# A hybrid convolution and attention block on one core: raw weights asked for two projections ahead, attention results in other slots, two rotation steps in front

## The chip, the core and the metric

The kernel runs on one core of a Trainium2 chip. What counts is the time of one execution on the device in microseconds (us), as the median of several runs. A core has five engines that run side by side, each with an instruction queue of its own: TensorE (PE in the profile, PEld for its weight loads), VectorE (DVE), ScalarE (ACT), GpSimd (POOL) and SyncE (SP), which here only issues DMA transfers. An instruction that waits holds up all that stand behind it on its engine.

## What is computed

The reference is a decoder block in float32 for 2048 tokens of width 1024:

```python
h = rmsnorm(x, norm_g[l])
proj = jnp.einsum("bsd,de->bse", h, w_in[l])
glu_in, conv_gate, q, k, v, attn_gate, merge_logits = jnp.split(proj, SPLIT_POINTS, axis=-1)
c = conformer_conv(glu_in, conv_dw_w[l], conv_dw_b[l], conv_ln_g[l], conv_ln_b[l])
y_conv = jnp.einsum("bsc,cd->bsd", c * jax.nn.silu(conv_gate), w_conv_out[l])
q = rope(q.reshape(B, S, N_Q_HEADS, HEAD_DIM), pos)
k = rope(k.reshape(B, S, N_KV_HEADS, HEAD_DIM), pos)
...
a = sliding_window_attention(q, k, v, sinks[l])
y_attn = jnp.einsum("bsa,ad->bsd", a * jax.nn.silu(attn_gate), w_attn_out[l])
g_conv, g_attn = jnp.split(jax.nn.sigmoid(merge_logits), 2, axis=-1)
x = x + jnp.einsum("bsd,de->bse", g_conv * y_conv + g_attn * y_attn, w_out[l])
return rmsnorm(x, final_norm_g)
```

(The gates' two lines are drawn into one here.) The convolution is a gated linear unit, a depthwise convolution over 31 tokens, a LayerNorm with scale and bias, and a SiLU. The attention has 16 query heads of 64 that share 4 key and value heads, a window of 128 tokens, and one sink per head in the softmax's denominator.

## The kernel before

**Sweeps and products.** The tokens are worked on in two sweeps of 1024, each as two halves of 512. Every float32 product is made of three matmuls in a rounded float32 form (`product`): a weight and an activation are each split into a rounded high part and what is left, the low part, and high x high, high x low and low x high are added up in PSUM. A projection (`project`) is one column group of 128 output columns: 2 halves x 8 slices of 128 inputs x 3 matmuls = 48 matmuls of 128x512. For the attention projection (names ya, on PE `mm_ya`), the convolution's (yc) and the gates (ag, cg, ma, mc) there are eight column groups each, written ya0_3 for sweep 0 and group 3. Queries come in pairs, q3_a and q3_b for the first and second half of the rotated vectors, ga and gb are the two inputs of the gated linear unit.

**Weights.** Each projection is an item with a prefetch and its blocks of matmuls. `Line.run` calls the prefetch of the next item and then runs the blocks of the held one, so the weights are asked for one item ahead. In `load_w` a group's weights come as two halves: SP issues the DMA of the raw weights (L273), ACT casts the high part (`whi`, L274), and in sweep 0 POOL makes the low part by a subtraction (`wlo`, L259), which is also stored to memory (`d_lo`, L290). In sweep 1 the low part is loaded from there (L276). The tiles raw, whi and wlo each have four buffers, that is, those of two projections.

**Order.** PE follows the program's order exactly. The other engines are ordered by a scheduler that knows priorities: `front()` (L326) lifts what is issued within it ahead of nearly all else, and the evacuation of a product from PSUM is lifted less. Three PSUM banks (`mm_ps`) take the projections' products in turn, so the fourth product can begin only when the first has been copied out.

**Slots.** Large tiles live in named slots: H and A for activations, C[0] to C[7] for the eight conv rows `cv`, X[0] to X[2] for three more. The DVE works on the convolution all through the projections; then comes its LayerNorm: the mean in X[0] (`ln_chain`, L934), `ln_chain2` (L946) with the reciprocal of the deviation in X[1], `ln_apply` (L930) with a multiply on DVE (L931) and a SiLU on ACT (L932) for each of the eight rows. `u_op` then multiplies row e, half by half, with its SiLU gate (`lcg`, L587) and splits the product into uT (cast L330 on ACT), the input of the convolution's projection; it notes ("u", e, half) as stored. X[2] is used by the attention's value tiles.

**The attention's projection.** `ya_item` evacuates column group e into mp[e], which takes the slot of conv row e. So it first lets the program issue all up to ("u", e, 1) (`line.until`), and its copies (L1037 on ACT) wait for the conv row to be used up. `yc_item` reads mp[e] (L1060), and the output projection's weights `wo` are loaded into C[0] to C[7] after that (`load_wo`, L1120).

**Queries and keys.** `rope_items` rotates them: `ev_a` and `ev_b` multiply a product by cosine and sine on DVE (tiles ra and rb, L603, L604, L609, L610), then POOL subtracts and adds (L611, L612), and the result is split (hq_a on ACT L652, hq_c on DVE L653) and stored to `d_q` by SP (L659), from where the attention loads it as `qk` (L755). The attention's scores (sc, L788) and its outputs (ov) lie on PE between the matmuls of the gates' projections; its normalized blocks are stored to `d_a`, and POOL's copies of the sinks into a block's tile (L794) wait for the stores of earlier ones.

Of the kernel before, what the change touches and what calls it, by code (L numbers as in the profile page):

```python
# [54 lines left out]
def hybrid_block(ctx: ExitStack, tc: tile.TileContext, x, xt, par_d, w_in, w_conv, sinks, w_attn, w_out,  # L55
# [202 lines left out]
    def split_lo(out_, full, hi, eng):  # L258
        return eng.tensor_tensor(out=out_, in0=full, in1=f(hi), op=ALU.subtract)  # L259

    def load_w(src, name, home=None, steps=None):

        parts = []
        at = lo_at.setdefault((src.tensor.name, src.offset), len(lo_at))

        def part(kh):
            if home is None:
                raw = stage.tile([P, 4, P], F32, tag="raw", name=f"raw_{name}{kh}")
                hi = stage.tile([P, 4, P], F32R, tag="whi", name=f"whi_{name}{kh}")
                lo = stage.tile([P, 4, P], F32R, tag="wlo", name=f"wlo_{name}{kh}")  # L270
            else:
                raw, hi, lo = (home[i][:, kh] for i in range(3))
            od(nc.sync.dma_start(out=raw, in_=src[:, 4 * kh:4 * kh + 4, :]))  # L273
            act.copy(hi, raw)  # L274
            if (at, kh) in lo_stored:
                od(nc.sync.dma_start(out=f(lo), in_=d_lo[at, kh]))  # L276
            else:
                split_lo(lo, raw, hi, dve if steps is not None else pool)
            parts.append((hi, lo))

        for kh in range(2):
            if steps is None:
                part(kh)
            else:
                steps.append(lambda kh=kh: part(kh))

        def keep(kh):
            if (at, kh) not in lo_stored:
                lo_stored.add((at, kh))
                nc.sync.dma_start(out=d_lo[at, kh], in_=f(parts[kh][1]))  # L290

        return lambda k: (parts[k // 4][0][:, k % 4, :], parts[k // 4][1][:, k % 4, :]), keep
# [9 lines left out]
    def project(src, rhs, name, evac, halves=(0, 1), small=False):  # L302

        got = {}

        def prefetch():
            got["w"] = load_w(src, name)

        def blocks():
            for half in halves:  # L310
                if small:
                    ps = small_bank(f"mm_{name}{half}")
                else:
                    ps = mm_ps.tile([P, TH], F32, tag="mm", name=f"mm_{name}{half}")
                for k in range(KC):
                    product(ps, got["w"][0](k), rhs(k, half), k)
                    if k == KC - 1:
                        with tc.high_priority(offset=PRIO):
                            evac(half, ps)
                    if half == halves[-1] and k % 4 == 3:  # L320
                        got["w"][1](k // 4)
                    yield 3 * MM_US

        return prefetch, blocks, (src, name, evac)

    def front():  # L326
        return tc.high_priority(offset=20 * PRIO)
# [175 lines left out]
    def sweep(s):  # L503
# [94 lines left out]
        def rope_items(name, e, store):  # L598
            first = {}

            def ev_a(half, ps):
                t = first[half] = slot(AT[4 + half], [P, 2, TH], F32, f"ra{s}_{name}_{half}")
                dve.tensor_tensor(out=t[:, 0, :], in0=ps, in1=cs[half][:, 0, :], op=ALU.mult)  # L603
                dve.tensor_tensor(out=t[:, 1, :], in0=ps, in1=cs[half][:, 1, :], op=ALU.mult)  # L604

            def ev_b(half, ps):
                a = first[half]
                b = slot(next_of("rb", [AT[6], AT[13]]), [P, 2, TH], F32, f"rb{s}_{name}_{half}")
                dve.tensor_tensor(out=b[:, 1, :], in0=ps, in1=cs[half][:, 1, :], op=ALU.mult)  # L609
                dve.tensor_tensor(out=b[:, 0, :], in0=ps, in1=cs[half][:, 0, :], op=ALU.mult)  # L610
                pool.tensor_tensor(out=a[:, 0, :], in0=a[:, 0, :], in1=b[:, 1, :], op=ALU.subtract)  # L611
                pool.tensor_tensor(out=a[:, 1, :], in0=a[:, 1, :], in1=b[:, 0, :], op=ALU.add)  # L612
                for i in range(2):
                    store(i, half, a[:, i, :])

            return [project(w_in[e], h_rhs, f"{name}a{s}", ev_a),
                    project(w_in[e + 1], h_rhs, f"{name}b{s}", ev_b)]
# [397 lines left out]
            glu_after = glu_after[2:]  # L1015
        for half in range(2):
            load_rope(half)
        for i, item in enumerate(others):
            todo = [item]
            if glu_after and i == glu_after[0]:  # L1020
# [3 lines left out]
                todo[0] = ahead(todo[0], start_attention)  # L1024
            if i == nqkv - 3:
                todo[0] = ahead(todo[0], prepare_v)
            yield from todo


        mp = {}  # L1030

        def ya_item(e, first):
            def ev(half, ps):
                if half == 0:
                    line.until(lambda: ("u", e, 1) in stored)
                    mp[e] = slot(C[e], [P, T], F32, f"mp{s}_{e}")
                act.copy(mp[e][:, half * TH:(half + 1) * TH], ps)  # L1037

            prefetch, blocks, _ = project(w_attn[e], lambda k, half: aT[half][k],
# [24 lines left out]

            return project(w_conv[e], lambda k, half: uT[half][k], f"yc{s}_{e}", ev)

        yield ya_item(0, True)
        for e in range(1, KC):
            yield ya_item(e, False)
        for e in range(KC):  # L1070
            yield yc_item(e)


        gb = work.tile([P, D], F32, tag="ln0", name=f"gb{s}", bufs=1)
# [182 lines left out]
```

## Time and profile before

| | us |
|---|---|
| median of 3 runs | 2004.92 (2004.77 to 2005.31) |
| the profiled execution's own time | 2003.76 |
| its span, first to last instruction | 2001.7 |
| PE busy | 1979.3 (99% of the span) |
| PEld busy | 1651.0 (82%) |
| DVE busy | 1305.1 (65%) |
| ACT busy | 982.1 (49%) |
| POOL busy | 434.3 (22%) |

The mean granted clock of TensorE was 0.996 of the full one. Rows of the timelines give the start and the duration in us, the engine, the line of the program, the operation with output and input names (buffer and group numbers left out), shapes, and how many instructions the row joins; brackets hold the idle time of the engine ahead of it and what ended that. A row "A <- B: total, times, longest" of the waits says that A waited for B. Matmuls are pipelined: a row of one can last 0.39 us while the next starts 0.23 us after it.

### The profile page before, as it was taken

How to read it: one execution, taken by the hardware profiler on the slowest of the kernel's cores; microseconds unless marked ns; L12 is line 12 of the kernel's file. 1: busy time of each engine (PE TensorE's matmuls, PEld its weight loads, DVE VectorE, ACT ScalarE, POOL GpSimd, SP SyncE). 2: the span in 40 equal slices, each digit the busy share in tenths (PEclk: the TensorE clock that was granted, in tenths of full speed). 3: DMA queues.
4: the chain of work that ended last, by engine and by line, in shares of the span. 5: the costliest groups of instructions: out<-in, count | busy, mean ns of one | idle time of the engine just before them, and what ended most of it. 6: DMA issues, size and time to landing. Idle time of an engine off the chain costs nothing.

```text
span 2001.7 us, 27128 instructions
## 1 busy us (share of the span) xinstructions
PE 1979.3 (99%) x9264; PEld 1651.0 (82%) x9264; DVE 1305.1 (65%) x1737; ACT 982.1 (49%) x2250; POOL 434.3 (22%) x462
## 2 busy tenths in 40 slices
PE   8999999999999998999999999999999999999998
PEld 6888788888888886888888888888888888888887
DVE  6998487787887546133858666787877875432434
ACT  7322567556555346234613126666565554553422
POOL 0445323423333242241001121111111110001200
PEclk9999999999999998999999999999999999999999
DMA  8566655655656844357537485556655677554632
GB/s 308 192 200 196 241 167 176 205 187 179 207 185 219 270 173 163 117 187 259 205 116 273 133 243 187 184 174 199 191 181 182 206 225 259 189 174 132 215 132 84
DMA packets 287545, 386.13 MB, mean 193 GB/s; under 512 B 22960, under 2 KB 138032, under 8 KB 287408
## 3 DMA queue, kind: packets, MB, share of 16 engines
q1 hardware_dynamic: 287408, 384.41, 57.7%
q8 instruction: 73, 1.20, 0.2%
q14 instruction: 64, 0.52, 0.1%
HBM read 252.20 MB, written 132.12 MB: 192 GB/s over the span
## 4 chain that ended last, share of the span: by engine, by line
PE 88%; DVE 1%; ACT 1%; SPq 0%; POOL 0%; DMA 0%; issue 0%; DVEq 0%; POOLq 0%; ACTq 0%
PE mm_cg L297 9%; PE mm_ma L297 9%; PE mm_mc L297 9%; PE o L1179 9%; PE mm_yc L297 9%; PE mm_ag L297 8%; PE mm_ya L297 8%; PE mm_ga L297 8%; PE mm_gb L297 7%; PE sc L788 3%; PE ov L847 2%; PE mm_q_a L297 2%; PE mm_q_b L297 2%; PE tpp L823 1%; PE mm_v L297 1%; PE mm_kb L297 1%
## 5 line engine op out<-in xcount | busy, mean ns | idle before, releaser
L526 DVE SCALAR_TENSOR_TENSOR acc<-glu,par,acc 128x1024 f32<-128x1024 f32 x464 | 595.6, 1284 | 7.4
L1179 PE MATMUL o<-wo,mT 128*128 128x512 f32 x768 | 174.8, 389 | 0.0
L1179 PEld LDWEIGHTS o<-wo,mT 128*128 128x128 f32 x768 | 144.2, 188 | 30.0
L297 PE MATMUL mm_ya<-aT,whi_ya 128*128 128x512 f32 x512 | 159.6, 393 | 7.5 <-ACT mp L1037 7.5
L297 PE MATMUL mm_cg<-hT,whi_cg 128*128 128x512 f32 x512 | 160.0, 394 | 0.0
L297 PE MATMUL mm_ma<-hT,whi_ma 128*128 128x512 f32 x512 | 160.0, 393 | 0.0
L297 PE MATMUL mm_ag<-hT,whi_ag 128*128 128x512 f32 x512 | 159.7, 393 | 0.0
L297 PE MATMUL mm_mc<-hT,whi_mc 128*128 128x512 f32 x512 | 158.3, 390 | 0.0
L297 PE MATMUL mm_yc<-uT,whi_yc 128*128 128x512 f32 x512 | 157.7, 389 | 0.0
L297 PE MATMUL mm_ga<-hT,whi_ga 128*128 128x512 f32 x448 | 139.7, 393 | 1.3 <-ACT whi_ga L274 1.3
L297 PE MATMUL mm_gb<-hT,whi_gb 128*128 128x512 f32 x448 | 139.5, 392 | 0.0
L811 ACT ACTIVATE ss<-ss,st 128x129 f32<-128x129 f32 x256 | 100.1, 394 | 60.7 <-DVE st L808 60.4
L297 PEld LDWEIGHTS mm_ya<-aT,whi_ya 128*128 128x128 f32 x512 | 97.1, 190 | 28.2 <-ACT mp L1037 7.9
L836 POOL TENSOR_SCALAR_AFFINE_SELECT pc<-pt 64x512 fp32r<-64x512 f32 x128 | 83.6, 654 | 153.2 <-ACT pt L831 141.9
L297 PEld LDWEIGHTS mm_yc<-uT,whi_yc 128*128 128x128 f32 x512 | 96.1, 188 | 19.9
L297 PEld LDWEIGHTS mm_mc<-hT,whi_mc 128*128 128x128 f32 x512 | 95.4, 188 | 19.5
L259 DVE TENSOR_TENSOR pt<-tpp,pt 128x512 fp32r<-128x512 f32 x64 | 44.2, 690 | 101.3 <-ACT pt L831 101.3
L297 PEld LDWEIGHTS mm_ag<-hT,whi_ag 128*128 128x128 f32 x512 | 93.5, 188 | 17.6
L297 PEld LDWEIGHTS mm_ma<-hT,whi_ma 128*128 128x128 f32 x512 | 93.0, 188 | 17.2
L297 PEld LDWEIGHTS mm_cg<-hT,whi_cg 128*128 128x128 f32 x512 | 93.0, 188 | 17.1
L1061 DVE TENSOR_TENSOR lmc<-mm_yc,lmc 128x512 f32<-128x512 f32 x32 | 22.0, 687 | 127.0 <-PE mm_yc L297 127.0
L297 PE MATMUL mm_ya<-aT,wlo_ya 128*128 128x512 f32 x256 | 100.3, 392 | 0.0
(450 smaller groups left out, 4332.0 us busy)
## 6 DMA issues: line engine op xcount, KB each, us to landing
qk<-d_q SPq DMA_DIRECT2D x64, 256.0 KB, 3.1
d_a<-ss SPq DMA_DIRECT2D x64, 256.0 KB, 3.4
aT<-d_a SPq DMA_DIRECT2D x32, 512.0 KB, 5.5
qk<-d_k SPq DMA_DIRECT2D x60, 256.0 KB, 4.0
d_k<-hlk SPq DMA_DIRECT2D x16, 512.0 KB, 4.4
d_q<-hq_c SPq DMA_DIRECT2D x16, 512.0 KB, 5.1
raw_ag<-in_w_in_dram SPq DMA_DIRECT2D x32, 256.0 KB, 4.6
d_ag<-ag SPq DMA_DIRECT2D x32, 256.0 KB, 2.5
```

The source lines that it names most:

```text
L259: return eng.tensor_tensor(out=out_, in0=full, in1=f(hi), op=ALU.subtract)
L297: pe.matmul(out=ps, lhsT=a, rhs=b, start=(k == 0 and i == 0), stop=(k == KC - 1 and i == 2))
L526: od(dve.scalar_tensor_tensor(out=to, in0=glu[c][:, j:j + T], scalar=tap(c, j), in1=acc[c], op0=ALU.mult, op1=ALU.add))
L788: pe.matmul(out=scs[qh][:, hp, c0:3 * HD], lhsT=w, rhs=k[:, qh + c0 // HD:qh + 3, j, :], start=(j == 0), stop=(j == 1))
L811: od(act.activation(out=ext[:, h, :], in_=ext[:, h, :], func=AF.Exp, bias=ngm[:, h:h + 1], accum_out=den[:, h:h + 1]))
L823: pe.transpose(out=tpp[:, h, :], in_=sb[:, h, :], identity=ident)
L836: pool.affine_select(out=pc[at], in_=f(pt[0:HD, a]), pattern=[[0, 2 * GQ], [1, HD]], compare_op=ALU.is_ge, fill=0.0, base=0, channel_multi ...
L847: pe.matmul(out=ov[:, cols], lhsT=vv, rhs=pp, start=(i == 0), stop=(i == len(seq) - 1))
L1061: dve.tensor_tensor(out=g, in0=ps, in1=g, op=ALU.mult)
L1179: pe.matmul(out=ps, lhsT=a[:, c0:c0 + P], rhs=r, start=(k == 0 and i == 0), stop=(k == KC - 1 and i == 2))
```

## The change

Three things are changed. First, a new helper `fetch_raw` allocates and loads a raw weight tile, a projection's prefetch gets a second part, `early`, that only asks for its raw tiles, and all items from the queries to the last convolution projection go into one list `flat`; each one's prefetch, through `linked`, also calls `early` of the item that follows. Raw weights are thus asked for two items ahead, casts and low parts stay one ahead. Second, mp[0] and mp[1] take X[2] and X[0], and mp[2] to mp[7] take C[0] to C[5]; `line.until` asks only for e > 1, and for ("u", e - 2, 1). Third, POOL's subtraction and addition of the rotation are issued within `front()`.

```diff
@@ -258,19 +258,24 @@
     def split_lo(out_, full, hi, eng):
         return eng.tensor_tensor(out=out_, in0=full, in1=f(hi), op=ALU.subtract)
 
-    def load_w(src, name, home=None, steps=None):
+    def fetch_raw(src, name, kh):
+        raw = stage.tile([P, 4, P], F32, tag="raw", name=f"raw_{name}{kh}")
+        od(nc.sync.dma_start(out=raw, in_=src[:, 4 * kh:4 * kh + 4, :]))
+        return raw
+
+    def load_w(src, name, home=None, steps=None, raws=None):
 
         parts = []
         at = lo_at.setdefault((src.tensor.name, src.offset), len(lo_at))
 
         def part(kh):
             if home is None:
-                raw = stage.tile([P, 4, P], F32, tag="raw", name=f"raw_{name}{kh}")
+                raw = raws[kh] if raws else fetch_raw(src, name, kh)
                 hi = stage.tile([P, 4, P], F32R, tag="whi", name=f"whi_{name}{kh}")
                 lo = stage.tile([P, 4, P], F32R, tag="wlo", name=f"wlo_{name}{kh}")
             else:
                 raw, hi, lo = (home[i][:, kh] for i in range(3))
-            od(nc.sync.dma_start(out=raw, in_=src[:, 4 * kh:4 * kh + 4, :]))
+                od(nc.sync.dma_start(out=raw, in_=src[:, 4 * kh:4 * kh + 4, :]))
             act.copy(hi, raw)
             if (at, kh) in lo_stored:
                 od(nc.sync.dma_start(out=f(lo), in_=d_lo[at, kh]))
@@ -303,8 +308,13 @@
 
         got = {}
 
+        def early():
+            got["raws"] = [fetch_raw(src, name, kh) for kh in range(2)]
+
         def prefetch():
-            got["w"] = load_w(src, name)
+            got["w"] = load_w(src, name, raws=got.get("raws"))
+
+        prefetch.early = early
 
         def blocks():
             for half in halves:
@@ -608,8 +618,9 @@
                 b = slot(next_of("rb", [AT[6], AT[13]]), [P, 2, TH], F32, f"rb{s}_{name}_{half}")
                 dve.tensor_tensor(out=b[:, 1, :], in0=ps, in1=cs[half][:, 1, :], op=ALU.mult)
                 dve.tensor_tensor(out=b[:, 0, :], in0=ps, in1=cs[half][:, 0, :], op=ALU.mult)
-                pool.tensor_tensor(out=a[:, 0, :], in0=a[:, 0, :], in1=b[:, 1, :], op=ALU.subtract)
-                pool.tensor_tensor(out=a[:, 1, :], in0=a[:, 1, :], in1=b[:, 0, :], op=ALU.add)
+                with front():
+                    pool.tensor_tensor(out=a[:, 0, :], in0=a[:, 0, :], in1=b[:, 1, :], op=ALU.subtract)
+                    pool.tensor_tensor(out=a[:, 1, :], in0=a[:, 1, :], in1=b[:, 0, :], op=ALU.add)
                 for i in range(2):
                     store(i, half, a[:, i, :])
 
@@ -1015,6 +1026,7 @@
             glu_after = glu_after[2:]
         for half in range(2):
             load_rope(half)
+        flat = []
         for i, item in enumerate(others):
             todo = [item]
             if glu_after and i == glu_after[0]:
@@ -1024,16 +1036,18 @@
                 todo[0] = ahead(todo[0], start_attention)
             if i == nqkv - 3:
                 todo[0] = ahead(todo[0], prepare_v)
-            yield from todo
+            flat += todo
 
 
         mp = {}
+        mp_tags = [X[2], X[0]] + C[0:6]
 
         def ya_item(e, first):
             def ev(half, ps):
                 if half == 0:
-                    line.until(lambda: ("u", e, 1) in stored)
-                    mp[e] = slot(C[e], [P, T], F32, f"mp{s}_{e}")
+                    if e > 1:
+                        line.until(lambda: ("u", e - 2, 1) in stored)
+                    mp[e] = slot(mp_tags[e], [P, T], F32, f"mp{s}_{e}")
                 act.copy(mp[e][:, half * TH:(half + 1) * TH], ps)
 
             prefetch, blocks, _ = project(w_attn[e], lambda k, half: aT[half][k],
@@ -1064,11 +1078,17 @@
 
             return project(w_conv[e], lambda k, half: uT[half][k], f"yc{s}_{e}", ev)
 
-        yield ya_item(0, True)
-        for e in range(1, KC):
-            yield ya_item(e, False)
-        for e in range(KC):
-            yield yc_item(e)
+        def linked(item, after):
+            def prefetch():
+                item[0]()
+                after[0].early()
+
+            return prefetch, item[1]
+
+        flat += [ya_item(e, e == 0) for e in range(KC)] + [yc_item(e) for e in range(KC)]
+        for item, after in zip(flat, flat[1:]):
+            yield linked(item, after)
+        yield flat[-1]
 
 
         gb = work.tile([P, D], F32, tag="ln0", name=f"gb{s}", bufs=1)
```

The order of PE's instructions is the same before and after. On POOL there is one place where the rotation moves, in sweep 0 at the query pairs q2 and q3. Before (ra0_q2__1 is the second half of pair 2, wlo_q3_b00 and b01 the low weights of pair 3's second projection):

```order
L611 TENSOR_TENSOR ra0_q2__0_1382<-ra0_q2__0_1382,rb0_q2__0_1469 128x512
L612 TENSOR_TENSOR ra0_q2__0_1382<-ra0_q2__0_1382,rb0_q2__0_1469 128x512
L259 TENSOR_TENSOR wlo_q3_b00_1533<-raw_q3_b00_1531,whi_q3_b00_1532 128x512
L259 TENSOR_TENSOR wlo_q3_b01_1539<-raw_q3_b01_1537,whi_q3_b01_1538 128x512
L611 TENSOR_TENSOR ra0_q2__1_1415<-ra0_q2__1_1415,rb0_q2__1_1516 128x512
L612 TENSOR_TENSOR ra0_q2__1_1415<-ra0_q2__1_1415,rb0_q2__1_1516 128x512
L259 TENSOR_TENSOR wlo_ag0_00_1606<-raw_ag0_00_1604,whi_ag0_00_1605 128x512
```

After:

```order
L622 TENSOR_TENSOR ra0_q2__0_1386<-ra0_q2__0_1386,rb0_q2__0_1473 128x512
L623 TENSOR_TENSOR ra0_q2__0_1386<-ra0_q2__0_1386,rb0_q2__0_1473 128x512
L622 TENSOR_TENSOR ra0_q2__1_1419<-ra0_q2__1_1419,rb0_q2__1_1520 128x512
L259 TENSOR_TENSOR wlo_q3_b00_1536<-raw_q3_b00_1432,whi_q3_b00_1535 128x512
L623 TENSOR_TENSOR ra0_q2__1_1419<-ra0_q2__1_1419,rb0_q2__1_1520 128x512
L259 TENSOR_TENSOR wlo_q3_b01_1540<-raw_q3_b01_1434,whi_q3_b01_1539 128x512
L259 TENSOR_TENSOR wlo_ag0_00_1609<-raw_ag0_00_1543,whi_ag0_00_1608 128x512
```

The subtraction (L622 is the old L611) of q2's second half has moved ahead of the first split of q3_b, and the addition (L623) ahead of the second.

On ACT the copies of the attention projection move. Sweep 0, before (cv0_0 to cv0_7 are the SiLUs of the conv rows, uT the casts of the convolution's result, mp0_0 the copies of column group 0):

```order
L932 ACTIVATE cv0_0_1323<-cv0_0_1323,par_81 128x1024
L932 ACTIVATE cv0_1_2024<-cv0_1_2024,par_81 128x1024
L932 ACTIVATE cv0_2_2758<-cv0_2_2758,par_81 128x1024
L932 ACTIVATE cv0_3_3512<-cv0_3_3512,par_81 128x1024
L932 ACTIVATE cv0_4_4253<-cv0_4_4253,par_81 128x1024
L932 ACTIVATE cv0_5_5001<-cv0_5_5001,par_81 128x1024
L932 ACTIVATE cv0_6_5754<-cv0_6_5754,par_81 128x1024
L932 ACTIVATE cv0_7_6438<-cv0_7_6438,par_81 128x1024
L330 CAST uT0_0_0_6949<-lcg0_0_0_7019 128x512
L330 CAST uT0_1_0_6957<-lcg0_0_1_7025 128x512
L1037 COPY mp0_0_7031<-mm_ya0_00_6965 128x512
L1037 COPY mp0_0_7031<-mm_ya0_01_7039 128x512
```

After, from the first gate activation (lcg) of the convolution on:

```order
L597 ACTIVATE lcg0_0_0_7115<-lcg0_0_0_7115 128x512
L1051 COPY mp0_0_7005<-mm_ya0_00_6969 128x512
L597 ACTIVATE lcg0_0_1_7145<-lcg0_0_1_7145 128x512
L597 ACTIVATE lcg0_1_0_7157<-lcg0_1_0_7157 128x512
L279 CAST whi_ya0_20_7041<-raw_ya0_20_6949 128x512
L597 ACTIVATE lcg0_1_1_7169<-lcg0_1_1_7169 128x512
L597 ACTIVATE lcg0_2_0_7187<-lcg0_2_0_7187 128x512
L279 CAST whi_ya0_21_7045<-raw_ya0_21_6951 128x512
L1051 COPY mp0_0_7005<-mm_ya0_01_7008 128x512
L943 ACTIVATE cv0_0_1327<-cv0_0_1327,par_81 128x1024
L943 ACTIVATE cv0_1_2028<-cv0_1_2028,par_81 128x1024
L943 ACTIVATE cv0_2_2762<-cv0_2_2762,par_81 128x1024
```

The copies of mp0_0 (L1051 is the old L1037) stood behind eight SiLUs and two casts, and now stand behind one and three gate activations, ahead of all SiLUs.

On SP the raw weights of the gated linear unit's third pair (raw_ga0_20 and 21) move. Before, up to the first of them (d_q are the stores of rotated queries, d_ag of a gate, qk the loads of the attention's first block):

```order
L659 DMA d_q_109<-hq0_2_0_a7_1481 128x8x128
L659 DMA d_q_109<-hq0_2_0_c2_1482 128x8x128
L659 DMA d_q_109<-hq0_2_2_a9_1485 128x8x128
L659 DMA d_q_109<-hq0_2_2_c4_1486 128x8x128
L659 DMA d_q_109<-hq0_2_3_a10_1525 128x8x128
L659 DMA d_q_109<-hq0_2_3_c5_1526 128x8x128
L755 DMA qk0_0_1765<-d_q_109 128x512
L758 DMA qk0_0_1765<-d_k_110 128x256
L659 DMA d_q_109<-hq0_2_1_a8_1521 128x8x128
L576 DMA d_ag_105<-ag0_0_0_1732 128x512
L659 DMA d_q_109<-hq0_2_1_c3_1522 128x8x128
L273 DMA raw_ga0_20_1775<-in_w_in_dram 128x512
```

After:

```order
L295 DMA d_lo_116<-wlo_q3_b00_1536 128x512
L295 DMA d_lo_116<-wlo_q3_b01_1540 128x512
L263 DMA raw_ga0_20_1702<-in_w_in_dram 128x512
L295 DMA d_lo_116<-wlo_ag0_00_1609 128x512
L263 DMA raw_ga0_21_1704<-in_w_in_dram 128x512
L295 DMA d_lo_116<-wlo_ag0_01_1613 128x512
L670 DMA d_q_109<-hq0_2_0_a7_1485 128x8x128
L670 DMA d_q_109<-hq0_2_0_c2_1486 128x8x128
L670 DMA d_q_109<-hq0_2_2_a9_1489 128x8x128
L670 DMA d_q_109<-hq0_2_2_c4_1490 128x8x128
L670 DMA d_q_109<-hq0_2_3_a10_1529 128x8x128
L670 DMA d_q_109<-hq0_2_3_c5_1530 128x8x128
```

The first request stood behind eight stores of queries, and both now stand ahead of them, between the stores of low weights.

## The prediction

> **What bounds the kernel now.** I read the page's busy row first (TensorE, PE, is busy for 99% of the span), then the list of what PE waited for, then the chain of work that ended last, then the timelines around each wait. With PE at 99% a change pays only where PE stands still, so the list of its waits comes first (columns: total, times, longest, in us).
>
> ```profile
> PE mm_ya L297 <- ACT mp L1037: 7.5, 1, 7.5
> PE mm_gb L297 <- ACT u_c L367: 6.3, 1, 6.3
> PE mm_ga L297 <- ACT whi_ga L274: 1.3, 1, 1.3
> PE mm_ga L297 <- DMA d_lo<-wlo_gb: 0.6, 1, 0.6
> ```
>
> There are four. The second is the start of the kernel, which the change leaves alone. The first is in sweep 0's attention projection (stall 1), the last two are one place in its projections for the gates (stall 2). The chain agrees: on both sides of stall 1 it is PE, and in between ScalarE (ACT).
>
> ```profile
> 736.07 2.73 PE mm_ya L297 x12
> 738.79 0.48 PE lnvar L907 x2
> ...
> 752.38 6.92 ACT cv L932 x6
> 760.86 73.26 PE mm_ya L297 x312
> 834.13 87.04 PE mm_yc L297 x384
> ```
>
> A matmul at full rate is thus 87.04 / 384 = 0.2267 us from start to start, and a projection's column group of 48 of them 10.88.
>
> **Part 1: where the attention projection's results go.** The timeline of PE around stall 1 (start, duration, operation):
>
> ```profile
> 752.98 0.39 PE L297 MATMUL mm_ya<-aT,wlo_ya 128*128 128x512 f32 x1
> 760.86 1.22 PE L297 MATMUL mm_ya<-aT,whi_ya 128*128 128x512 f32 x2 [7.50 <-ACT mp L1037]
> 761.88 0.63 PE L297 MATMUL mm_ya<-aT,wlo_ya 128*128 128x512 f32 x1
> 762.31 1.05 PE L297 MATMUL mm_ya<-aT,whi_ya 128*128 128x512 f32 x2
> ...
> 765.93 0.40 PE L297 MATMUL mm_ya<-aT,whi_ya 128*128 128x512 f32 x1
> ```
>
> Rows alternate between one and two matmuls, so 13 start from 752.98 up to 765.93. At full rate they need 13 x 0.2267 = 2.95 us and they took 12.95: stall 1 costs 10.0 us. The gap itself is 752.98 + 0.23 to 760.86, 7.65; the other 2.35 are the matmuls behind it, which start 0.43 apart (761.88 to 762.31) until about 765.7.
>
> ACT's timeline in the same stretch says why:
>
> ```profile
> 743.61 3.13 ACT L587 ACTIVATE lcg<-lcg 128x512 f32<-128x512 f32 x5
> ...
> 752.38 6.92 ACT L932 ACTIVATE cv<-cv,par 128x1024 f32<-128x1024 f32 x6 [1.00 <-DVE cv L931]
> 759.21 1.12 ACT L330 CAST uT<-lcg 128x512 fp32r<-128x512 f32 x2
> 760.24 1.06 ACT L1037 COPY mp<-mm_ya 128x512 f32<-128x512 f32 x2
> ```
>
> The copy of the first result (mp) needs the slot of conv row 0, and so stands behind all eight SiLUs of the conv rows and two casts that consume row 0. Only then does its PSUM bank come free for the fourth product. With the change mp of column group 0 takes an attention tile's slot and waits for no conv row; in the order it stands behind one lcg activation. With 3.13 / 5 = 0.63 us for that one, the copy starts at about 743.6 + 0.6 = 744.2 and ends near 744.8. The fourth product is due at 752.98 + 0.23 = 753.2, so the bank is free 8 us early. The gap and the slow matmuls behind it go: **-10.0 us**.
>
> What is late next on ACT? The copies of groups 0 and 1, 1.06 / 2 = 0.53 each, now lie among the conv SiLUs: three ahead of the last one, which ended at 752.38 + 6.92 = 759.3 and ends by 760.9. Behind it come one copy, one uT cast (1.12 / 2 = 0.56) and the two casts of group 3's weights, 0.62 each by the row of the cast in part 2: done by 763.3. PE without the stall begins group 3 at 736.07 + 0.48 + 3 x 10.88 = 769.2, so 6 us cover the casts, and GpSimd's splits behind them (1.29 each by the rows of part 3) keep some 4.5. The copy of group 2's first half now waits for conv row 0 to be used up, near 763; its product ends at 763.8 and its bank is wanted again three products of 5.44 later, less one, at 774.6: 10 us of cover. I cost these follow-ons at nothing; if GpSimd needs more than the 4.5, the price is what the first rival says. Sweep 1 has no wait at this place in the list above, so nothing is won there.
>
> At the other end of the slots the output projection's weights (wo) take the conv rows' slots. That of wo 5 is now given back by mp of group 7, whose last reading was
>
> ```profile
> 916.55 0.69 DVE L1060 TENSOR_TENSOR lma<-mp,lma 128x512 f32<-128x512 f32 x1 [0.76 <-ACT lma L587]
> ```
>
> at 917.24. The output projection begins at 834.13 + 87.04 = 921.2 and wants wo 5 five steps of three matmuls later, at 924.6: 7 us for a cast (0.62) and a split, so nothing is added.
>
> **Part 2: raw weights asked for two projections ahead.** The rows of PE, SyncE's queue (SP), ACT and GpSimd (POOL) around stall 2, each from its own timeline:
>
> ```profile
> 207.85 0.39 PE L297 MATMUL mm_gb<-hT,wlo_gb 128*128 128x512 f32 x1
> 209.58 0.73 PE L297 MATMUL mm_ga<-hT,whi_ga 128*128 128x512 f32 x2 [1.33 <-ACT whi_ga L274]
> 210.94 0.50 PE L297 MATMUL mm_ga<-hT,wlo_ga 128*128 128x512 f32 x1 [0.63 <-DMA d_lo<-wlo_gb]
> 211.28 1.00 PE L788 MATMUL sc<-qk 128*128 128x64 f32 x8
> ```
>
> ```profile
> 202.97 1.30 SPq L273 DMA_DIRECT2D raw_ga<-in_w_in_dram  x1
> ```
>
> ```profile
> 208.91 0.62 ACT L274 CAST whi_ga<-raw_ga 128x512 fp32r<-128x512 f32 x1 [8.76 <-DMA raw_ga<-in_w_in_dram]
> ```
>
> ```profile
> 209.60 2.56 POOL L259 TENSOR_TENSOR wlo_ga<-raw_ga,whi_ga 128x512 fp32r<-128x512 f32 x2 [10.87 <-ACT whi_ga L274]
> ```
>
> The weights of one projection (ga) are asked for at 202.97, by the old order right behind the last of the stores of rotated queries; they arrive some 5.9 us later, when the cast starts (208.91), the cast ends at 209.5, and PE was ready at 208.1. Four matmuls took 211.28 - 207.85 = 3.43 us for 4 x 0.2267 = 0.91: stall 2 costs 2.5 us, and no slow matmuls follow it. In the changed order the request stands ahead of all eight stores, right behind the stores of the low parts of q3's weights, so it goes out near 180 (part 3 has these low parts ready by 179.9) and not at 203. ACT and GpSimd had been idle for 8.76 and 10.87 us: they can do the cast and the splits before PE asks: **-2.5 us**.
>
> Over the rest of the kernel two requests per projection move ahead of other requests on SP, each about half of the 1.30 that the request at 202.97 took at most. Queued behind them are the stores of low parts, the attention's loads and, through these, PE's scores; the last rival prices that. What they win elsewhere is nothing: PE's list holds no other wait for weights, so ACT's earlier casts only lengthen a cover that is already there.
>
> **Part 3: rotation's GpSimd steps in front.** Priority moves one such step and changes one place: the subtraction of q2's second half now stands ahead of the split of q3's low weights (wlo_q_b), the addition between its two halves. Before:
>
> ```profile
> 170.23 3.35 POOL L259 TENSOR_TENSOR wlo_q_b<-raw_q_b,whi_q_b 128x512 fp32r<-128x512 f32 x2
> 174.36 1.29 POOL L611 TENSOR_TENSOR ra_q__1_1415<-ra_q__1_1415,rb_q__1_1516 128x512 f32<-128x512 f32 x1 [0.78 <-DVE rb_q__1_1516 L609]
> ```
>
> ```profile
> 170.87 1.55 DVE L653 SCALAR_TENSOR_TENSOR hq_c<-ra_q__0_1382,hq_a 128x512 fp32r<-128x512 f32 x1
> 173.54 0.68 DVE L609 TENSOR_TENSOR rb_q__1_1516<-mm_q_b,cs 128x512 f32<-128x512 f32 x1
> 177.60 0.69 DVE L653 SCALAR_TENSOR_TENSOR hq_c<-ra_q__1_1415,hq_a 128x512 fp32r<-128x512 f32 x1 [0.15 <-ACT hq_a L652]
> ```
>
> ```profile
> 175.43 0.61 PE L297 MATMUL mm_q_b<-hT,whi_q_b 128*128 128x512 f32 x2
> 175.89 0.39 PE L297 MATMUL mm_q_b<-hT,wlo_q_b 128*128 128x512 f32 x1
> 178.61 0.39 PE L297 MATMUL mm_q_b<-hT,wlo_q_b 128*128 128x512 f32 x1
> ```
>
> The subtraction waits for VectorE's product (ends 174.22), so it can't run before 174.36. It ends at 175.65; the split then takes 1.29 (as the other POOL rows) to 1.7 (half of 3.35): first low part ready at 176.9 to 177.3, where PE wants it at 175.89. PE would stand for 1.0 to 1.4 us. The other end: as the split does not run at 170.9, VectorE's hq_c may take 0.69 in place of 1.55 and all that follows it, the product too, comes 0.86 earlier: then 0.15 to 0.55 us. The second low part, behind the addition and 1.29 of its own, is ready 2.6 us after the first (179.5 to 179.9 at worst) and wanted 2.72 us after it: covered. Bounds 0.15 and 1.4; I take **+0.7 us**, nearer to the second case, because the row of hq_c that is nearest to what 170.87 becomes is the one at 177.60, with no split beside it (0.69). The gap is shorter than stall 2's 1.33, behind which PE went on at full rate, so I add no slow matmuls.
>
> **The sum.** -10.0 - 2.5 + 0.7 = -11.8. The profiled execution took 2003.76 us (span 2001.7), so it would become 1992.0; it lies 1.16 below the median of the three runs shown, 2004.92, so against that I forecast 2004.92 - 11.8 = **1993.1 us**. With the ends of part 3 it would be 1992.6 or 1993.8.
>
> **Rivals.** What a measurement of this kernel can tell from no change is about 0.2%, 4.0 us: faster is below 2000.9, slower above 2008.9.
>
> *GpSimd held out by VectorE.* One row in which a pair of splits takes far more than 2.6, while VectorE subtracts in SBUF without a pause:
>
> ```profile
> 702.33 8.88 POOL L259 TENSOR_TENSOR wlo_mc<-raw_mc,whi_mc 128x512 fp32r<-128x512 f32 x2 [7.45 <-ACT whi_mc L274]
> ```
>
> ```profile
> 702.91 3.48 DVE L922 TENSOR_TENSOR cv<-cv,mu 128x1024 f32<-128x1024 f32 x3
> ```
>
> So one split took up to 8.88 - 1.29 = 7.6 us. In the q3 place the split now starts at 175.65 between VectorE's two hq_c (to 178.29). If it is held until the second ends, it is done at 178.29 + 1.29 = 179.6, 3.7 after PE wants it: the sum becomes -8.8, 1996.1, or 1998.5 with the slow matmuls of stall 1 (2.35) behind it; rows show them behind a gap of 7.65 us and not behind 1.33, and nothing between. If the whole 7.6 is met there, or at group 3 of the attention projection: 183.3 - 175.9 = 7.4 and the 2.35: the sum is -12.5 + 9.75 = -2.75, 2002.2. Against: POOL's row at 174.36 kept 1.29 beside VectorE's work. The Trainium skill, "SBUF — State Buffer", section "Who interferes with whom", has this as a rule: a VectorE instruction with two SBUF inputs and a GpSimd instruction that reads SBUF exclude each other for a whole instruction. By that rule the split would be held here and the sum would be the -8.8 in place of -11.8; the 702.33 row agrees with it, the 1.29 row does not. The Trainium skill, "TensorE: Matmul & The Clock Gate", section "Part 1: The HAM clock gate", puts half rate behind an idle window of about 3.4 us; by that a gap of 3.7 is on the edge and 1998.5 possible. Chance 0.08, three parts in four of it at 1996.1 to 1998.5.
>
> *Another wait takes stall 1's place.* The copies of groups 2 and later still need a conv row (two back), and ACT has the SiLUs, 16 uT casts and copies in one queue. If one bank comes free 3 to 5 us late, the sum is -9 to -7: 1996 to 1998. For it: ACT works without a pause from 752.38. Against: the row that a copy now waits for is two groups older, and each group is 10.88 us on PE. Chance 0.10.
>
> *Stall 2 stays.* If the early request waits for a raw buffer until 203 all the same: -9.3, 1995.6. Chance 0.06.
>
> *The gain does not arrive.* PE is done earlier but the copy still waits, since its new slot, an attention tile's, is not free: then only -2.5 + 0.7 = -1.8, 2003.1. Against: by the program's order attention's products all stand ahead of this projection's. Chance 0.06.
>
> *Slower: SP's queue blocks.* A request two ahead waits for a raw buffer that a split must give back; on SP the attention's loads and stores (qk, d_a) queue behind it, and POOL already waits for those:
>
> ```profile
> POOL ss L794 <- DMA d_a<-ss: 326.0, 46, 12.6
> qk<-d_q SPq DMA_DIRECT2D x64, 256.0 KB, 3.1
> 208.37 0.46 SPq L755 DMA_DIRECT2D qk<-d_q  x1
> 225.11 1.03 PE L788 MATMUL sc<-qk 128*128 128x192 f32 x8
> ```
>
> The second block's queries are asked for at 208.37, land 3.1 later at 211.5, and are used at 225.11: 13.6 us to spare. It decides once SP stands still for longer than that. With 14 us in all 64 blocks, 0.4 each, it costs 25.6: 25.6 - 11.8 = +13.8, 2018.7. The longest wait of the list is 12.6, so it needs more than anything in this trace. Chance 0.04.
>
> **Chances.** The forecast 0.66 and the five rivals 0.08, 0.10, 0.06, 0.06, 0.04. Faster: 0.66 + 0.10 + 0.06 + 0.08 (all but its last case) = 0.88; within 0.2%: 0.06 and 0.02 = 0.08; slower 0.04. The range starts at 1991.8, the lower end of part 3 (1992.6) less 0.8 (between the 0.54 that the three runs shown spread and the 1.16 from profile to median), and reaches through both rivals with part of the gain to 1998.0; outside lie 0.06 + 0.04 and about 0.04 of the first rival.
>
> **What would show it.** Right: no PE wait on mp in the list, the fourth product of the attention projection follows the third at full rate, mp's first copy near 744, raw_ga issued before 190 and no wait for whi_ga, and one new PE wait of under 1.5 us on wlo_q_b near 176. Wrong: a new PE wait of over 3 us between 750 and 835, a split of wlo_q_b or wlo_ya of over 3 us, or the scores (sc) waiting for qk.

## The result

The changed kernel takes 1991.99 us (median of 4 runs, 1991.75 to 1992.64), the kernel before in the same series 2005.12. The ratio is 0.9934, 95% interval 0.9917 to 0.9951: 13.1 us faster, where 11.8 were forecast. The profiled executions took 2003.76 before and 1991.75 after, 12.0 apart.

The list of what PE waited for in the changed kernel (total, times, longest, in us) shows both stalls gone and one new wait:

```profile
PE mm_gb L302 <- ACT u_c L377: 5.7, 1, 5.7
PE mm_q_b L302 <- DVE ra_q__0_1573 L614: 0.4, 1, 0.4
```

Its chain of work runs through the attention projection without leaving PE:

```profile
733.95 2.73 PE mm_ya L302 x12
736.67 0.93 PE lnvar L918 x4
737.61 84.36 PE mm_ya L302 x372
821.97 87.04 PE mm_yc L302 x384
```

The 372 matmuls take 84.36 / 372 = 0.2268 us each, full rate, where stall 1 had been. ACT's timeline shows the copies at their new places, the first one 16.7 us earlier than before (760.24):

```profile
742.96 0.63 ACT L597 ACTIVATE lcg<-lcg 128x512 f32<-128x512 f32 x1
743.49 0.57 ACT L1051 COPY mp<-mm_ya 128x512 f32<-128x512 f32 x1
...
757.55 0.57 ACT L1051 COPY mp<-mm_ya 128x512 f32<-128x512 f32 x1
758.01 0.63 ACT L340 CAST uT<-lcg 128x512 fp32r<-128x512 f32 x1
758.53 1.15 ACT L279 CAST whi_ya<-raw_ya 128x512 fp32r<-128x512 f32 x2
```

The last two rows are what was feared to be late next: group 3's weights are cast by 759.7, and GpSimd's row behind them splits both by 762.4, while PE begins group 3 near 767.5 (12 matmuls by 736.67, the other 132 from 737.61 on).

```profile
759.24 3.13 POOL L259 TENSOR_TENSOR wlo_ya<-raw_ya,whi_ya 128x512 fp32r<-128x512 f32 x2 [8.96 <-ACT whi_ya L279]
```

At the place of stall 2, SP's requests, ACT's casts, GpSimd's splits and PE's first products:

```profile
179.79 0.33 SPq L263 DMA_DIRECT2D raw_ga<-in_w_in_dram  x1
...
181.04 0.33 SPq L263 DMA_DIRECT2D raw_ga<-in_w_in_dram  x1
...
189.95 0.37 SPq L670 DMA_DIRECT2D d_q<-hq_a  x1
```

```profile
199.88 1.13 ACT L279 CAST whi_ga<-raw_ga 128x512 fp32r<-128x512 f32 x2
```

```profile
200.57 2.54 POOL L259 TENSOR_TENSOR wlo_ga<-raw_ga,whi_ga 128x512 fp32r<-128x512 f32 x2 [1.52 <-ACT whi_ga L279]
```

```profile
208.20 0.39 PE L302 MATMUL mm_gb<-hT,wlo_gb 128*128 128x512 f32 x1
208.43 0.61 PE L302 MATMUL mm_ga<-hT,whi_ga 128*128 128x512 f32 x2
208.88 0.39 PE L302 MATMUL mm_ga<-hT,wlo_ga 128*128 128x512 f32 x1
```

The requests go out at 179.79 and 181.04, ahead of the query stores, the low parts are ready at 203.1, and PE goes from one product to the next in 0.23 us at 208.4.

The new cost, at the third query pair, in the rows of GpSimd, ACT, VectorE and PE:

```profile
172.56 1.30 POOL L622 TENSOR_TENSOR ra_q__1_1419<-ra_q__1_1419,rb_q__1_1520 128x512 f32<-128x512 f32 x1 [3.33 <-DVE rb_q__1_1520 L619]
173.81 1.29 POOL L259 TENSOR_TENSOR wlo_q_b<-raw_q_b,whi_q_b 128x512 fp32r<-128x512 f32 x1
175.06 1.74 POOL L623 TENSOR_TENSOR ra_q__1_1419<-ra_q__1_1419,rb_q__1_1520 128x512 f32<-128x512 f32 x1
176.76 1.30 POOL L259 TENSOR_TENSOR wlo_q_b<-raw_q_b,whi_q_b 128x512 fp32r<-128x512 f32 x1
```

```profile
176.84 0.63 ACT L663 ACTIVATE hq_a<-ra_q__1_1419 128x512 fp32r<-128x512 f32 x1 [2.32 <-POOL ra_q__1_1419 L623]
```

```profile
172.93 1.28 DVE L536 SCALAR_TENSOR_TENSOR acc<-glu,par,acc 128x1024 f32<-128x1024 f32 x1
174.55 1.10 DVE L664 SCALAR_TENSOR_TENSOR hq_c<-ra_q__1_1419,hq_a 128x512 fp32r<-128x512 f32 x1 [0.34 <-ACT hq_a L663]
177.50 1.11 DVE L664 SCALAR_TENSOR_TENSOR hq_c<-ra_q__1_1419,hq_a 128x512 fp32r<-128x512 f32 x1 [1.85 <-ACT hq_a L663]
...
180.33 0.67 DVE L614 TENSOR_TENSOR ra_q__0_1573<-mm_q_a,cs 128x512 f32<-128x512 f32 x1
```

```profile
174.47 0.61 PE L302 MATMUL mm_q_b<-hT,whi_q_b 128*128 128x512 f32 x2
175.16 0.50 PE L302 MATMUL mm_q_b<-hT,wlo_q_b 128*128 128x512 f32 x1
...
180.29 0.39 PE L302 MATMUL mm_q_b<-hT,wlo_q_b 128*128 128x512 f32 x1
181.06 0.74 PE L302 MATMUL mm_q_b<-hT,whi_q_b 128*128 128x512 f32 x2 [0.38 <-DVE ra_q__0_1573 L614]
...
186.67 0.62 PE L302 MATMUL mm_ag<-hT,whi_ag 128*128 128x512 f32 x2
```

The 48 matmuls of q3's second projection take 186.67 - 174.47 = 12.20 us in place of 10.88: 1.3 us lost. Only 0.24 of it is the wait for the first low part (175.16, due 0.45 behind 174.47). The largest piece is 180.29 to 181.06, 0.54 more than a step: a PSUM bank. GpSimd's addition, now between the splits, ends at 176.80; ACT's hq_a and VectorE's hq_c wait for it in their queues, and behind hq_c, and one more step of the convolution (acc), stands the product (180.33 to 181.00) that empties the bank.

So the profiled executions differ by -10.0 (stall 1), -2.5 (stall 2) and +1.3, together -11.2. PE's first matmul came 0.6 earlier (its wait at the start is 5.7 and not 6.3), which in the runs below is chance from run to run (5.3 to 6.3). These make -11.8 of the 12.0; the small rest was not followed.

### The profile page after: what moved, and what is told of

Its sections match the earlier page's. It is cut to its first block, busy times and chain, and to the rows that moved or that the text cites. A ratio compares the mean times of both kernels' runs of the same rounds, so it can differ in the third digit from the quotient of the medians.

```text
span 1990.0 us, 27146 instructions
## 1 busy us (share of the span) xinstructions
PE 1976.9 (99%) x9264; PEld 1649.1 (83%) x9264; DVE 1309.2 (66%) x1737; ACT 982.7 (49%) x2250; POOL 429.9 (22%) x462
## 4 chain that ended last, share of the span: by engine, by line
PE 91%; DVE 0%; ACT 0%; POOL 0%; issue 0%
PE mm_cg L302 9%; PE mm_ma L302 9%; PE mm_ag L302 9%; PE mm_mc L302 9%; PE o L1199 9%; PE mm_ya L302 9%; PE mm_yc L302 9%; PE mm_ga L302 8%; PE mm_gb L302 8%; PE sc L799 3%; PE mm_q_b L302 2%; PE ov L858 2%; PE mm_q_a L302 2%; PE tpp L834 1%; PE mm_v L302 1%; PE mm_kb L302 1%
## 5 line engine op out<-in xcount | busy, mean ns | idle before, releaser
L302 PE MATMUL mm_cg<-hT,wlo_cg 128*128 128x512 f32 x256 | 100.0, 391 | 0.0
L302 PE MATMUL mm_ma<-hT,wlo_ma 128*128 128x512 f32 x256 | 100.0, 391 | 0.0
```

The lines of the kernel that those rows point to most:

```text
L302: pe.matmul(out=ps, lhsT=a, rhs=b, start=(k == 0 and i == 0), stop=(k == KC - 1 and i == 2))
```

## The experiments

The new wait was put down to the third part, GpSimd's rotation steps in front. The first four kernels take the change apart to test that and the sum; the others ask which piece of a part is needed. The times, with the ratio to the kernel before in the same series:

| kernel | median us, runs (range) | ratio, 95% interval |
|---|---|---|
| without the priority | 1991.57, 5 (1991.08 to 1992.87) | 0.9931 (0.9918 to 0.9943) |
| slots only | 1994.52, 5 (1994.06 to 1995.38) | 0.9945 (0.9932 to 0.9959) |
| raw weights only | 2001.48, 11 (2000.91 to 2002.30) | 0.9979 (0.9970 to 0.9988) |
| priority only | 2005.23, 11 (2002.77 to 2006.49) | 0.9999 (0.9990 to 1.0008) |
| before, in the series of these four | 2004.76, 21 (2003.45 to 2008.59) | |
| one group back, no priority | 1992.34, 5 (1991.63 to 1993.57) | 0.9939 (0.9925 to 0.9953) |
| new slots, old condition, no priority | 1991.84, 5 (1991.77 to 1992.36) | 0.9935 (0.9923 to 0.9948) |
| early from the gates on, no priority | 1990.76, 5 (1990.09 to 1992.41) | 0.9930 (0.9917 to 0.9942) |
| before, in the series of these three | 2004.93, 9 (2003.93 to 2006.29) | |
| one projection early, no priority | 1991.18, 5 (1989.47 to 1992.28) | 0.9929 (0.9917 to 0.9942) |
| the change again | 1992.07, 5 (1991.05 to 1992.52) | 0.9933 (0.9919 to 0.9947) |
| before, in the series of these two | 2005.51, 9 (2003.96 to 2005.97) | |

**Without the priority.** The changed kernel less its third part:

```diff
-                with front():
-                    pool.tensor_tensor(out=a[:, 0, :], in0=a[:, 0, :], in1=b[:, 1, :], op=ALU.subtract)
-                    pool.tensor_tensor(out=a[:, 1, :], in0=a[:, 1, :], in1=b[:, 0, :], op=ALU.add)
+                pool.tensor_tensor(out=a[:, 0, :], in0=a[:, 0, :], in1=b[:, 1, :], op=ALU.subtract)
+                pool.tensor_tensor(out=a[:, 1, :], in0=a[:, 1, :], in1=b[:, 0, :], op=ALU.add)
```

> The changed kernel without the priority on the rotation's two GpSimd steps. Theory: the three parts add up and the priority alone costs the steps seen at the third query pair in the changed kernel's trace, 1.2 us (0.35 at its first low part, 0.18 at its second, 0.65 at the next PSUM bank); so about 1990.8 against 1992.0, with only the wait at the start left on the list of PE's waits. Rival: the priority also brings the query stores forward and is part of what ends stall 2; then without it a wait of 1 to 2.5 us on whi_ga or wlo_ga comes back near 208, 1992 to 1994.5.

Both were wrong. The time, 1991.57, is not told apart from the change's, and the wait at the third query pair is still there, the same size:

```profile
PE mm_gb L302 <- ACT u_c L377: 5.4, 1, 5.4
PE mm_q_b L302 <- DVE ra_q__0_1573 L614: 0.4, 1, 0.4
```

The order says why: with and without the priority the instructions of all five engines stand in the same order, row for row. The third part does nothing; the moved subtraction must come from another part.

**Slots only.** The first and third part are undone, the new slots stay:

```diff
             def prefetch():
                 item[0]()
-                after[0].early()
```

> Of the change only the slots of the attention projection's results. Theory: -10.0 against the kernel before, 1995.1, stall 2 still there with 2.5 us. Rival: the attention projection without its stall also needs raw weights earlier, and without them a new wait on weights of 1 to 4 us comes at its groups 3 or 4: 1996 to 1999.

The theory holds: 10.2 below the kernel before (2004.76), nothing new in the attention projection, stall 2 still there, the third query pair without a wait.

```profile
PE mm_gb L302 <- ACT u_c L377: 5.8, 1, 5.8
PE mm_ga L302 <- ACT whi_ga L279: 2.0, 1, 2.0
PE mm_ga L302 <- POOL wlo_ga L259: 0.6, 1, 0.6
```

**Raw weights only.** The early requests stay, slots and condition are the old ones:

```diff
-        mp_tags = [X[2], X[0]] + C[0:6]
+        mp_tags = C
...
-                    if e > 1:
-                        line.until(lambda: ("u", e - 2, 1) in stored)
+                    line.until(lambda: ("u", e, 1) in stored)
```

> Of the change only the raw weights asked for two projections ahead. Theory: -2.5 against the kernel before, 2002.6, stall 1 unchanged at 10 us. Rival: earlier weights also let the casts move ahead of the copies elsewhere, or requests in SyncE's queue hold up the attention's loads: then 2004 or more, with waits of PE on qk or on copies that the kernel before did not have.

```profile
PE mm_ya L302 <- ACT mp L1049: 7.5, 1, 7.5
PE mm_gb L302 <- ACT u_c L377: 6.0, 1, 6.0
PE mm_q_b L302 <- DVE ra_q__0_1573 L614: 0.4, 1, 0.4
```

Stall 2 is gone, stall 1 stays, no wait on qk: as the theory has it. But the wait at the third query pair is here too, without the priority. So it comes with the early raw weights, whose tiles and requests the scheduler sees earlier. The gain, 3.3 us (0.9970 to 0.9988 is 6.0 to 2.4), is the price of stall 2 less these 1.3, if stall 1 cost the same; in this kernel's trace stall 1 took 9.3 (763.22 - 751.67 for ten matmuls that need 2.27) and not 10.0. The two kernels with the new slots, which have no stall 1, point the same way: slots only less the first experiment is 1994.52 - 1991.57 = 2.95, and with the 1.3 again more than the 2.5 of the one profiled execution. So stall 2 cost more in these runs; the next kernel shows how that can be.

**Priority only.** The kernel before with its GpSimd steps in front, as in the change's third part.

> Of the change only the priority on the rotation's GpSimd steps. Theory: +1.2 against the kernel before, 2006.3, a wait near 175 to 181 at the third query pair. Rival: it brings the query stores and with them the raw weights behind them forward; then stall 2 shrinks by up to 2.5 and the time is 2004 to 2005.5.

No change (0.9990 to 1.0008), and no wait at the third query pair: the theory falls, and the reading of the first experiment is confirmed from the other side. The time, 2005.23, lies within the rival's 2004 to 2005.5, but the rival falls too, since stall 2 has not shrunk. Its profiled execution, 2006.49, was the slowest of its 11, and shows what stall 2 can do:

```profile
207.98 0.39 PE L302 MATMUL mm_gb<-hT,wlo_gb 128*128 128x512 f32 x1
210.28 0.73 PE L302 MATMUL mm_ga<-hT,whi_ga 128*128 128x512 f32 x2 [1.91 <-ACT whi_ga L279]
211.63 0.50 PE L302 MATMUL mm_ga<-hT,wlo_ga 128*128 128x512 f32 x1 [0.62 <-POOL wlo_ga L259]
211.97 1.00 PE L799 MATMUL sc<-qk 128*128 128x64 f32 x8
212.81 1.07 PE L302 MATMUL mm_ga<-hT,whi_ga 128*128 128x512 f32 x2
213.68 0.63 PE L302 MATMUL mm_ga<-hT,wlo_ga 128*128 128x512 f32 x1
...
216.50 0.39 PE L302 MATMUL mm_ga<-hT,whi_ga 128*128 128x512 f32 x1
```

From 207.98 to 211.97 four matmuls took 3.99 us in place of 0.91, 3.1 lost. The nine from 212.81 to 216.50 took 3.69 in place of 2.04, 1.65 more: half rate (granted clock 0.51 from 212.8 to 216.2), without a long gap ahead. The same two gaps in the kernel with the slots only lost 212.01 - 207.88 - 0.91 = 3.2 and had no slow matmuls behind them (granted clock 1.00 in the same stretch; the last row is cut by the end of the window):

```profile
207.88 0.39 PE L302 MATMUL mm_gb<-hT,wlo_gb 128*128 128x512 f32 x1
210.32 0.74 PE L302 MATMUL mm_ga<-hT,whi_ga 128*128 128x512 f32 x2 [2.05 <-ACT whi_ga L279]
211.67 0.50 PE L302 MATMUL mm_ga<-hT,wlo_ga 128*128 128x512 f32 x1 [0.62 <-POOL wlo_ga L259]
212.01 1.00 PE L798 MATMUL sc<-qk 128*128 128x64 f32 x8
212.85 0.45 PE L302 MATMUL mm_ga<-hT,whi_ga 128*128 128x512 f32 x1
```

So stall 2 cost 2.5, 3.2 and 3.1 + 1.65 = 4.75 us in three executions. That fits the gain of the raw weights alone; that it explains the scatter of the kernel before (2003.45 to 2008.59) is argued from these three traces, not shown run by run.

**One group back.** Only group 0 gets an attention tile's slot (no priority):

```diff
-        mp_tags = [X[2], X[0]] + C[0:6]
+        mp_tags = [X[2]] + C[0:7]
...
-                    if e > 1:
-                        line.until(lambda: ("u", e - 2, 1) in stored)
+                    if e > 0:
+                        line.until(lambda: ("u", e - 1, 1) in stored)
```

> The changed kernel without the priority, and with only group 0's result in an attention tile's slot; every later one takes the conv row one group back. Theory: the stall came from group 0's copy alone, and group 1's bank is wanted only two products later, near 764, by when conv row 0 is used up (about 762 in the kernel before); so no wait of over 1 us and the same time as the first experiment, 1991.6. Rival: two groups back are needed, since the copy of group 1 stands behind six SiLUs and two casts and is late: a wait of 1 to 4 us on mp near 762, 1992.5 to 1996.

No wait on mp in its list, and the time is not told apart from the change's. The copies of group 1 stand behind six SiLUs and the two casts of row 0, as the rival had it, but the last two SiLUs come behind them, and they are not late. In ACT's timeline they run at

```profile
755.87 0.58 ACT L1050 COPY mp<-mm_ya 128x512 f32<-128x512 f32 x1
...
757.50 0.57 ACT L1050 COPY mp<-mm_ya 128x512 f32<-128x512 f32 x1
```

so one extra slot is enough.

**New slots, old condition.** The slots of the change, but each copy is issued only when row e has been used up, as before (no priority):

```diff
-                    if e > 1:
-                        line.until(lambda: ("u", e - 2, 1) in stored)
+                    line.until(lambda: ("u", e, 1) in stored)
```

> The changed kernel without the priority, and with the old condition on when a copy is issued (row e used up) but the new slots. Theory: the slot is what held the copy, not the order in which the program issues; group 0's copy runs near 745 and the time is that of the first experiment, 1991.6. Rival: the order of issue holds it; then the copies of group 0 or 1 stand late in ScalarE's queue and a wait of 1 to 8 us on mp comes back, 1993 to 2001.

The slot is what held the copy. Although it is issued later in the program, in ACT's timeline it runs at

```profile
744.56 0.57 ACT L1049 COPY mp<-mm_ya 128x512 f32<-128x512 f32 x1
```

and no wait on mp is in the list; 1991.84.

**Early requests from the gates on.** With the slots and without the priority, the requests two ahead are left out for the query, key and value projections:

```diff
         for i, item in enumerate(others):
...
             flat += todo
+            if i < nqkv:
+                no_early += [t[0] for t in todo]
...
-                after[0].early()
+                if after[0] not in no_early:
+                    after[0].early()
```

> New slots, no priority, raw weights two ahead from the first gate projection on, not among the queries. GpSimd keeps the old order at the third query pair, all later requests are early as in the change. Theory: the same as the kernel with one early projection, 1990.5, within 0.5: the other early requests neither win nor cost. Rival: the many requests ahead of the attention's loads on SyncE's queue cost something, 0.5 to 2 us more than with one place; or they win something, 1990 or less.

1990.76, and for the first time the start is the only wait of PE:

```profile
PE mm_gb L302 <- ACT u_c L377: 5.8, 1, 5.8
```

GpSimd has the old order back, the split of both low parts ahead of the subtraction:

```profile
169.59 3.35 POOL L259 TENSOR_TENSOR wlo_q_b<-raw_q_b,whi_q_b 128x512 fp32r<-128x512 f32 x2
173.72 1.29 POOL L621 TENSOR_TENSOR ra_q__1_1415<-ra_q__1_1415,rb_q__1_1516 128x512 f32<-128x512 f32 x1 [0.78 <-DVE rb_q__1_1516 L619]
```

So it is the early requests among the queries that brought the new wait. Why the scheduler moves the subtraction for them was not followed.

**One projection early, and the change again.** Only the ga of sweep 0's third pair is asked for two ahead, with the slots and without the priority; the changed kernel itself runs in the same rounds.

```diff
         for i, item in enumerate(others):
...
                 todo = glu_items(KC - 1 - len(glu_after)) + todo
+                if s == 0 and not alone:
+                    alone.append(todo[1][0])
...
-                after[0].early()
+                if after[0] in alone:
+                    after[0].early()
```

> New slots, no priority, and raw weights asked for two ahead for one single projection, the ga of the third pair in sweep 0. GpSimd's order is then that of the kernel before. Theory: all of the gain of the early raw weights lies in this one place (stall 2, 3.2 us in the run with the slots only), and the wait at the third query pair (1.1 us) comes with the early requests of the query projections; so neither stall, as in the kernel with early requests from the gates on, 1990.8. Rival: early requests elsewhere carry part of the gain, and without them the time is 1991.6 or more.

> The changed kernel itself, on the same chip and in the same rounds as the kernel with one early projection. Theory: 1.1 us above that one, 1992.0. Rival: the two can't be told apart, within 0.5.

1991.18 against 1992.07. One early projection does all that the early requests of the whole kernel do: its wait list has the start alone, in two rows (5.3 and 0.3 us). That it is the better kernel by about 1 us is what its trace says, which lacks the wait of 1.3. The runs of one kernel spread by 1 to 3 us, so that single kernels are hard to tell apart by their times; but in these two series the ten runs of the two kernels without the wait average 1991.0 and the fifteen of the three with it 1992.1, and the difference of 1.1 is uncertain by about 0.7.

## Why the prediction was right, and where not

**Stall 1, -10.0: right.** Slots alone brought 10.2. The mechanism is the one named, the copy held by its slot: the old condition with the new slots made no wait. The cover of what comes next (casts, splits, group 2's copy, wo) held everywhere. Of the 10.0, the 2.35 of slow matmuls is the part that changes from run to run: 1.6 and 3.0 in the two other traces that have this stall.

**Stall 2, -2.5: right in the mechanism, its size from one execution too small.** Other traces showed 3.2 and 4.75 for it. The forecast from the median (2004.92) less terms from a profiled execution 1.16 faster than that median took stall 2 at its cheapest. With part 3 at its real size the terms make 11.2, so 1.9 of the measured 13.1 is not in them; dearer executions of stall 2, and of the slow matmuls behind stall 1, can hold it, which is not shown run by run. The rest of the early requests win nothing, as said: one place does it.

**Part 3: the failed step is "Priority moves one such step and changes one place".** The move was read off the order of the whole change and put down to the part that names those instructions. The runs show that the priority moves nothing, and that the early raw weights of the query projections moved the subtraction. The place was right. That the loss, 1.3, is within the bounds of 0.15 and 1.4 is luck, for the bounds were drawn for the first low part alone, which cost 0.24 in its wait; the second was called covered, and the PSUM bank behind VectorE's hq_c, behind the addition that was moved too, was not in the sum. So the sign named for it, a wait on wlo_q_b in PE's list, did not come: the list names VectorE's product, that is, the bank. There is luck in the total as well: 1991.99 lies 0.2 above the lower end of the range, because a loss taken 0.6 too small made up for part of a gain taken 1.9 too small.

**The rivals.** The first one, GpSimd held out by VectorE, came true in small, and the prediction had misread it. At the third query pair three instructions were each issued while one of the other engine still ran, and took longer than alone: hq_c at 174.55 took 1.10 in place of 0.69 (the split beside it had 0.55 to go, to 175.10), the addition at 175.06 took 1.74 in place of 1.29 (hq_c had 0.59 to go), and hq_c at 177.50 took 1.11 (the second split had 0.56 to go). The Trainium skill, "SBUF — State Buffer", section "Who interferes with whom", has a VectorE instruction with two SBUF inputs and a GpSimd instruction that reads SBUF exclude each other for the whole of one; the trace agrees: each was stretched by 0.41 to 0.45, nearly what was left of the other. Beside VectorE's acc (172.93 to 174.21) the subtraction and the split kept their 1.30 and 1.29, but acc adds to a tile in PSUM (`cv_ps` in the kernel) and so has only one input from SBUF. The row at 174.36, which the prediction held against the rule, is no evidence either: what ran beside it, products of mm_q_b and acc, has an input in PSUM too. What was wrong in the price of 3.7 is the length: the split was never held until both hq_c were done.

Two of these holds, 0.45 and 0.42, lie on the way to the PSUM bank. Without them VectorE's product would end near 181.00 - 0.87 = 180.13, before PE wants the bank at 180.29 + 0.23 = 180.52; and the second low part, which only the first of them delays, would be ready at 178.06 - 0.45 = 177.61, before PE wants it at 177.59 + 0.45 = 178.04. By this estimate the wait for the bank, the largest piece of the 1.3, comes of the two engines holding each other up; no run was made that takes the holds alone away.

No other wait came in the attention projection, and SP's queue held up no scores: the list of none of these kernels has a wait on qk.

## What to carry to other kernels

When a change has several parts, build each alone and compare the orders before putting a moved instruction down to one: here the part that named it moved nothing, and a part about DMA requests moved it. When an engine's step is moved between two others, follow all that wait for it, down to the PSUM bank that PE wants next, and look which instructions of VectorE and GpSimd then meet, and where their inputs lie. An evacuation that shares its slot with a tile still in use waits for all work on that tile; one spare slot for the first result took away a 10 us stall on an engine that is busy for 99% of the time.

## What the hardware showed that was not expected

Half rate can follow a short gap, and what it costs depends on when the slow stretch ends. With 1.91 and 0.62 us of idle time a little apart, PE ran nine matmuls at half rate in one execution, beginning 2.5 us after the longer gap had ended; with 2.05 and 0.62 us in another, none. The Trainium skill, "TensorE: Matmul & The Clock Gate", section "Part 1: The HAM clock gate", speaks of an idle window of about 3.4 us and of one that runs freely. The slow stretch here, 212.81 to some 216.2, is of that length; an idle stretch as long did not precede it. What decides between the two executions was not tried. Behind stall 1's gap of 7.5 us slow matmuls followed in every trace that had it: 1.6 us worth in the kernel with the raw weights only, 2.35 in the kernel before and 3.0 in the one with the priority only. In these three traces the granted clock is at half for 6.83, 10.24 and 10.24 us, two and three times the 3.41 of the short stretch, and it begins inside the gap. What of it was left when PE went on (762.81 - 759.55 = 3.3, 765.64 - 760.86 = 4.8 and 769.26 - 763.14 = 6.1) ran at half rate, and half of that was lost.
